# A transformer block on one Trainium2 core: gate 1 in four column groups per step, gate 2 summed by VectorE during the down projections

## The chip, the cores and the metric

The kernel runs on one core of one Trainium2 chip. The metric is the device time of one execution in microseconds (us); the kernel before took 1503.56 us, the median of three runs. The core has five instruction streams that matter here: PE (TensorE, the matrix engine; PEld is its weight load), DVE (VectorE), ACT (ScalarE), POOL (GpSimd) and SP, whose stream issues all the large loads from HBM.

## What is computed

One layer of a diffusion transformer on 256 latent tokens of width 2048, with 256 context tokens. A vector `c` gives six modulation vectors of 2048 each. The layer mixes the tokens by three branches (hyena, retention, S5), projects the result, adds it through gate `m_lat[2]`, and then does the same with a convolutional feed-forward network (FFN) through gate `m_lat[5]`:

```python
m_lat = jnp.split((jax.nn.silu(c) @ ada_w[i] + ada_b[i])[:, None, :], N_MOD, axis=-1)
a_lat = _modulate(h_lat, norm1_g[i], m_lat[0], m_lat[1]) @ w_in[i]
...
mix_l = jnp.concatenate([hyena_l, retention_l, s5_l], axis=-1) @ w_out[i]
h_lat = h_lat + m_lat[2] * mix_l
h_lat = h_lat + m_lat[5] * _conv_ffn(_modulate(h_lat, norm2_g[i], m_lat[3], m_lat[4]), ...)
return _rmsnorm(h_lat, norm_f)
```

`ada_w` has 2048 rows and 6 x 2048 columns. Of its six chunks of 2048 columns the first two are used for norm 1. The other four are what the change is about: `m_lat[2]` is chunk 0 of the kernel's `ada25` (gate 1), `m_lat[3]` and `m_lat[4]` are chunks 1 and 2 (shift and scale of norm 2), and `m_lat[5]` is chunk 3 (gate 2).

## The kernel before

Activations lie with features on the 128 partitions and the 256 tokens along the free dimension. All weights are float32 and come in blocks of 256 rows by 512 columns (512 KB). Each block is loaded by SP into a page of the ring `raw`, cast by ACT to its high part in a page of the ring `wh` (L454), and the remainder is taken by DVE into a page of `wl` (L456, called the split below). PE then makes three products per tile (L461, L462, L463: high by high, high by low, low by high), 24 matmuls of 256 columns per block in the usual case.

The order of work is this. Norm 1 and the S5 input come first, as the first two chunks of the modulation arrive (L373). Then follow keys and values with the S5 scan beside them, gate and queries, the three hyena projections with retention and the hyena transforms beside them, the output projection by `w_out`, and the FFN. The FFN has 11 units; `up(u)` takes 16 blocks of `w_up`, and `down(g)` takes the blocks of `w_down` for a group of two units (16 blocks, the last group 8). `down` runs over four column groups `cg` of 512 output features. The FFN runs in the order up 0, up 1, up 2, down 0, up 3, up 4, down 1 and so on, with down 5 last. After each column group of `down`, four DVE operations multiply the sums in PSUM by gate 2 and add them to the residual `hres` (L1419).

The four later chunks are made by the task `t_ada` (`ada25`), a generator that is advanced by a rate after every weight block: RK and RV (2 and 3 steps) during keys and values, RG and RH (0.8) during gate, queries and hyena, RW (0.75) during the output projection, RF (0.8) in `up`. A chunk is 32 loads of 512 KB (16 row tiles, two halves). It is made in one of two ways. `ada_matmul` (chunks 0 and 3) keeps `silu(c)` as the weights, 32 columns wide, and streams the chunk through PE in float32: four products per row tile, one for each 32-partition group of one PSUM bank (L412). Its task yields after each half, so that two products are emitted at a step. `ada_vector` (chunks 1 and 2, the list ADV) lets DVE scale and add the rows' tiles (L428, L430) and needs PE for four products at the end (L435). Both end in `ada_store`: an ACT copy (L363), four transposes on PE (L397) and a DVE addition (L400) into `ada_cols`. The loads go through the ring `ada`, which has two pages from the keys on (the first entry of RN); `raw`, `wh` and `wl` have three pages then, and four in the FFN.

The text order is not the executed order. A scheduler takes the emitted operations with their priorities, simulates the engines and lays down one instruction order per engine; on the chip every engine and SP run in that order. The splits of the weights have priority (PW).

Of the kernel before, what the change touches and what calls it, by code (L numbers as in the profile page):

```python
# [16 lines left out]
P = 128  # L17
# [39 lines left out]
def _lay(i):  # L57
    """The inputs as the kernel reads them: slices, transposes and constants of the shapes."""
# [84 lines left out]
    # constants of the shapes  # L143
# [24 lines left out]
RN=[2,3,3,3];SA=40000;SF=30000;R0=10;R1=1;R2=1;RS=4;RK=2;RV=3;RG=.8;RH=.8;RW=.75;RF=.8;RT=1.2;RR=3;RY=.75;PR=500;ADV=[1,2];ORD=[0,1,2,3];RP=1.5;RQ=20;KS=5;PW=800;AR=[6,8,8,8,7,5,5,5];ZE=[1,3];VE=[0,1,3];UE=[1,3]  # L168
class _Pages:
    """Tags of fixed sizes in the slot pool, taken and given back in the order of the program."""  # L170
# [12 lines left out]
class _Ring:  # L183
    """Tags taken in turn."""
# [9 lines left out]
class _Task:  # L194
    """Work that is emitted piece by piece between the blocks of the large products."""
# [23 lines left out]
def tile_dit(ctx: ExitStack, tc: tile.TileContext, I, out: bass.AP, dbg=None):  # L219
# [14 lines left out]
    @contextmanager  # L234
    def stream(name, start):
        """Instructions whose order of priority starts at -start and goes on from use to use."""
        n = counts.get(name, 0)
        with tc.high_priority(offset=tc.cur_priority + start - n):
            before = tc.cur_priority
            yield  # L240
            counts[name] = n + tc.cur_priority - before
# [4 lines left out]
    def resize(kind, n):  # L246
        """A ring of n pages of 4 KB."""
# [58 lines left out]
    def sum_squares(ps, sq, first, last):  # L306
        """Sums over the partitions and parts of sq [P, n, w], a token on each partition."""
# [6 lines left out]
    def inv_rms(ps, n, w):  # L314
        """1/sqrt(sum/n + eps) of w tokens' sums, on all partitions."""
# [76 lines left out]
    def ada_store(c, ps):  # L392
        """Four rows of 512 columns to their places."""
# [10 lines left out]
    def ada_matmul(c):  # L404
        """2048 of the modulation's columns for the latents, as products of TensorE."""
        ps = ada_bank()
        for kt in range(KT):
            raw = [load_a(I["ada25"][c, kt, half]) for half in range(2)]
            for half in (1, 0):
                for e in range(2):  # L410
                    q = 2 * half + e
                    T.matmul(ps[32 * q:32 * q + 32, :], cs[:, kt, :], raw[half][:, e, :],  # L412
                             start=(kt == 0), stop=(kt == KT - 1), skip_group_check=True)
                if (kt, half) != (KT - 1, 0):
                    yield
# [3 lines left out]
    def ada_vector(c):  # L419
        """The same, summed over the rows' tiles by VectorE and over partitions by TensorE."""  # L420
        ps = ada_bank()
        for half in range(2):
            tag = pages.take(4)
            acc = slot(tag, [P, 2, 512])
            for kt in range(KT):
# [5 lines left out]
                if kt < KT - 1:  # L431
                    yield
            for e in range(2):
# [4 lines left out]
            if half == 0:  # L438
                yield
# [3 lines left out]
    def ada25():  # L443
        """The other four chunks of the modulation (2048 columns each), for the latents."""
        for c in ORD:
            yield from (ada_vector if c in ADV else ada_matmul)(c)

# [11 lines left out]
    def prod(ps, a, b, first, last):  # L459
        """ps += a.T @ b with a = (high, low), b = (high, low)."""  # L460
# [12 lines left out]
    def feat_block(src, k0, at, mv, first, last):  # L473
        """256 rows of the weights into 512 features' sums: a bank's first start clears it for both."""
# [27 lines left out]
    def hyena_filters():  # L502
# [36 lines left out]
        for o in range(2):  # L539
            # even and odd parts of the filter's lags  # L540
# [833 lines left out]
    def with_ada():  # L1374
        t_ada.run(RF)
# [99 lines left out]
```

## Time and profile before

| | us |
|---|---|
| runs | 1507.85, 1503.56, 1503.34 |
| median of the runs | 1503.56 |
| profiled execution: its span | 1506.4 |
| PE busy | 1459.1 (97%) |
| DVE busy | 1040.6 (69%) |
| ACT busy | 658.0 (44%) |
| matmuls of L412 (chunks 0 and 3), busy | 62.7 |
| DVE sums of L430 (chunks 1 and 2), busy | 76.8 |

The profile gives the span of its execution and no time around it; that span is 2.8 us (0.2%) above the median of the runs. Busy time of an engine is the union of its instructions; a matmul's recorded duration overlaps that of the next one, so the pace of PE is read from starts, not from durations. A float32 product stands in the trace as two matmuls, and in the order of instructions as one row. The profile's chain is the sequence of work that ended last, followed back from the end.

### The profile page before, as it was taken

The numbers are of one execution on the slowest core, as the hardware profiler recorded it, in microseconds if no ns is written. First come the engines' busy times: TensorE is split into PE (matmuls) and PEld (weight loads), VectorE is DVE, ScalarE is ACT, GpSimd is POOL, SyncE is SP. The second block draws the span as 40 slices with busy tenths as digits, with TensorE's granted clock in tenths as the row PEclk, the third lists the DMA queues.
The fourth block names the chain that finished last, engine by engine and source line by source line (L and its number), as shares of the span: only waits on it lengthen the run. The fifth ranks groups of instructions, "written<-read, shape, count | busy, mean of one in ns | idle before, by whom it ended". The sixth has DMA issues, their size and how long they took to land.

```text
span 1506.4 us, 27320 instructions
## 1 busy us (share of the span) xinstructions
PE 1459.1 (97%) x11180; PEld 1314.7 (87%) x11180; DVE 1040.6 (69%) x1772; ACT 658.0 (44%) x974; POOL 10.9 (1%) x9
## 2 busy tenths in 40 slices
PE   6998999999999999999999999999999999999997
PEld 3566687678888987788899999999999999999997
DVE  6579519897869887653777665775667577657756
ACT  6337741213576433232554443443444344434434
POOL 0000000000000000000000000000000000000000
PEclk9999999999999999999999999999999999999998
DMA  9788635568877887677465666556665666656562
GB/s 352 260 313 291 229 101 197 183 194 278 281 252 253 299 303 261 219 226 251 145 182 183 185 182 184 185 177 192 183 183 182 182 183 183 185 183 184 178 189 90
DMA packets 89956, 318.58 MB, mean 211 GB/s; under 512 B 12039, under 2 KB 12584, under 8 KB 89384
## 3 DMA queue, kind: packets, MB, share of 16 engines
q1 hardware_dynamic: 89832, 316.85, 65.4%
q8 instruction: 87, 1.43, 0.4%
q14 instruction: 37, 0.30, 0.1%
HBM read 312.62 MB, written 4.19 MB: 210 GB/s over the span
## 4 chain that ended last, share of the span: by engine, by line
PE 83%; DVE 7%; DMA 5%; ACT 3%; issue 1%; SPq 0%; DVEq 0%; ACTq 0%
PE mm L461 24%; PE mm L462 23%; PE mm L463 23%; DMA s4k<-in_ada_dram 4%; PE ad L412 4%; DVE s4k L456 1%; DVE s4k L430 1%; PE sm L852 1%; PE ad L373 1%; PE sm L576 1%; PE mm L339 1%; PE sm L546 1%; DMA s4k<-in_x_t_dram 1%; PE sm L1158 0%; PE sm L1164 0%
## 5 line engine op out<-in xcount | busy, mean ns | idle before, releaser
L456 DVE TENSOR_TENSOR s4k<-s4k,s4k 128x1024 fp32r<-128x1024 f32 x376 | 459.6, 1223 | 324.1 <-ACT s4k L454 300.5
L454 ACT CAST s4k<-s4k 128x1024 fp32r<-128x1024 f32 x376 | 393.8, 1048 | 654.7 <-PE mm L462 483.3
L462 PE MATMUL mm<-s4k,s4k 128*128 128x256 f32 (+1 forms) x2144 | 629.0, 294 | 1.5 <-DVE s4k L775 1.2
L461 PE MATMUL mm<-s4k,s4k 128*128 128x256 f32 (+1 forms) x2144 | 626.9, 295 | 3.5 <-ACT s4k L454 3.1
L463 PE MATMUL mm<-s4k,s4k 128*128 128x256 f32 (+1 forms) x2144 | 624.7, 294 | 3.2 <-DVE s4k L456 3.2
L461 PEld LDWEIGHTS mm<-s4k,s4k 128*128 128x128 f32 x2144 | 411.9, 193 | 27.3 <-issue 12.9
L462 PEld LDWEIGHTS mm<-s4k,s4k 128*128 128x128 f32 x2144 | 414.3, 193 | 18.4 <-issue 8.2
L463 PEld LDWEIGHTS mm<-s4k,s4k 128*128 128x128 f32 x2144 | 412.1, 193 | 17.2 <-issue 6.9
L461 PE MATMUL mm<-s8k,s4k 128*128 128x256 f32 x960 | 272.7, 285 | 0.0
L462 PE MATMUL mm<-s8k,s4k 128*128 128x256 f32 x960 | 271.7, 284 | 0.0
L463 PE MATMUL mm<-s8k,s4k 128*128 128x256 f32 x960 | 271.1, 284 | 0.0
L461 PEld LDWEIGHTS mm<-s8k,s4k 128*128 128x128 f32 x960 | 183.9, 192 | 14.4 <-issue 12.6
L463 PEld LDWEIGHTS mm<-s8k,s4k 128*128 128x128 f32 x960 | 183.7, 192 | 4.3 <-issue 3.4
L462 PEld LDWEIGHTS mm<-s8k,s4k 128*128 128x128 f32 x960 | 184.3, 192 | 2.7 <-issue 2.5
L1396 DVE SCALAR_TENSOR_TENSOR t<-mm,s4k,t 128x189 f32<-128x189 f32 (+2 forms) x352 | 131.9, 424 | 7.9 <-ACT t L1388 6.3
L430 DVE SCALAR_TENSOR_TENSOR s4k<-s4k,cs,s4k 128x1024 f32<-128x1024 f32 x60 | 76.8, 1280 | 21.0 <-DMA s4k<-in_ada_dram 20.4
L412 PE MATMUL ad<-s4k,cs 128*32 128x512 f32 x256 | 62.7, 612 | 1.0 <-DMA s4k<-in_ada_dram 1.0
L1419 DVE SCALAR_TENSOR_TENSOR s4k<-mm,ada_cols,s4k 128x256 f32<-128x256 f32 x96 | 39.9, 477 | 4.7 <-PE mm L463 4.7
L373 PE MATMUL ad<-s4k,cs 128*32 128x256 f32 x512 | 35.6, 392 | 4.7 <-DMA s4k<-in_ada_dram 4.0
L1388 ACT ACTIVATE t<-mm,s4k 128x256 f32<-128x256 f32 x44 | 24.7, 562 | 14.6 <-PE mm L463 13.6
L466 ACT CAST s8k<-t 128x512 fp32r<-128x512 f32 x38 | 23.0, 616 | 18.2 <-DVE t L1403 9.3
L373 PEld LDWEIGHTS ad<-s4k,cs 128*32 128x32 f32 x512 | 13.8, 110 | 19.1 <-DMA s4k<-in_ada_dram 5.7
(281 smaller groups left out, 1023.5 us busy)
## 6 DMA issues: line engine op xcount, KB each, us to landing
s4k<-in_ada_dram SPq DMA_DIRECT2D x192, 512.0 KB, 4.9
s4k<-in_w_up_dram SPq DMA_DIRECT2D x176, 512.0 KB, 3.7
s4k<-in_w_down_dram SPq DMA_DIRECT2D x88, 512.0 KB, 3.7
s4k<-in_w_in_dram SPq DMA_DIRECT2D x80, 512.0 KB, 4.9
s4k<-in_w_out_dram SPq DMA_DIRECT2D x32, 512.0 KB, 4.6
s4k<-in_x_t_dram SPq DMA_DIRECT2D x8, 512.0 KB, 6.6
s4k<-in_ctx_t_dram SPq DMA_DIRECT2D x4, 512.0 KB, 10.2
hyk<-s8k SPq DMA_DIRECT2D x4, 512.0 KB, 4.0
```

What stands on the lines that cost most here:

```text
L373: T.matmul(ps[32 * q:32 * q + 32, :], cs[:, 2 * k2 + e, :], raw[:, e, 256 * part:256 * part + 256], start=(k2 == 0), stop=(k2 == 7), skip_ ...
L412: T.matmul(ps[32 * q:32 * q + 32, :], cs[:, kt, :], raw[half][:, e, :], start=(kt == 0), stop=(kt == KT - 1), skip_group_check=True)
L430: V.scalar_tensor_tensor(acc, raw, cs[:, kt, 0:1], acc, ALU.mult, ALU.add)
L454: S.copy(h, raw)
L456: V.tensor_tensor(lo, raw, h.bitcast(F32), ALU.subtract)
L461: T.matmul(ps, a[0], b[0], start=first, stop=False, skip_group_check=True)
L462: T.matmul(ps, a[0], b[1], start=False, stop=False, skip_group_check=True)
L463: T.matmul(ps, a[1], b[0], start=False, stop=last, skip_group_check=True)
L466: S.copy(h, src)
L1388: S.activation(acc[:, e, :], at(m), AF.Identity, bias=cw[:, 9, mt:mt + 1], scale=cw[:, 4, mt:mt + 1])
L1396: V.scalar_tensor_tensor(dst[:, r0:r1, c0:c1], src[:, r0 + dy:r1 + dy, c0 + dx:c1 + dx], cw[:, tap, mt:mt + 1], dst[:, r0:r1, c0:c1], ALU. ...
L1419: V.scalar_tensor_tensor(h_of(mt), at(m), ada_cols[:, 3, mt:mt + 1], h_of(mt), ALU.mult, ALU.add)
```

## The change

Four things are changed; comments and doc strings are dropped besides.

- Chunk 0 (`ada_matmul`) emits the four products of a row tile together, in the order of the column groups 0 to 3, and yields twice.
- Chunk 3 leaves `t_ada`, which makes chunks 0 to 2 alone and is finished ahead of the second norm. Chunk 3 is now a task of its own, `t_gate`, made by `ada_vector` on DVE, advanced by RD = 0.5 after each block of `down`. A one-element copy from `dsum` ties its sums to the first result of down 0. `ada_vector` yields twice more between its last sum and its products.
- The results of down 0 to down 4 are no longer gated one by one. Down 0's are copied by ACT into two buffers `dsum` of 8 KB per partition, those of down 1 to 4 are added to them by DVE, 512 columns at a time. Ahead of down 5 the sums are gated once, in 16 DVE operations; down 5 is gated as before.
- Retention emits the score products of both heads of a pair together, alternating between the two halves of the partitions, into two PSUM banks.

```diff
 def ada_matmul(c):
-            for half in (1, 0):
-                for e in range(2):
-                    q = 2 * half + e
-                    T.matmul(ps[32 * q:32 * q + 32, :], cs[:, kt, :], raw[half][:, e, :], ...)
-                if (kt, half) != (KT - 1, 0):
-                    yield
+            for q in range(4):
+                T.matmul(ps[32 * q:32 * q + 32, :], cs[:, kt, :], raw[q // 2][:, q % 2, :], ...)
+            if kt < KT - 1:
+                yield
+                yield
+        yield
...
-    def ada_vector(c):
+    def ada_vector(c, after=None):
...
+            if after is not None:
+                V.tensor_copy(acc[:, 0, 0:1], after)
...
+            yield
+            yield
...
-        for c in ORD:
+        for c in range(3):
...
+            pss = [sm_bank(), sm_bank()]
+            for s in range(2):
+                for e in range(2):
+                    ph = slice(64 * e, 64 * e + 64)
+                    T.matmul(pss[e][:, L * s:L * s + L], k_t[ph, pr, 128 * s:128 * s + 128], q_t[ph, pr, :], ...)
...
+    t_ada.finish()
     r = inv_rms(sums, D, L)
...
+    dsum = [slot(pages.take(8), [P, 8, L]) for _ in range(2)]
...
-    def with_ada():
-        t_ada.run(RF)
+    t_gate = _Task(ada_vector(3, dsum[0][:, 0, 0:1]))
+    def with_down(g, cg):
+        if (g, cg) != (0, 0):
+            t_gate.run(RD)
+    def gated(cg):
+        for mt in range(4 * cg, 4 * cg + 4):
+            V.scalar_tensor_tensor(h_of(mt), dsum[cg // 2][:, mt % 8, :], ada_cols[:, 3, mt:mt + 1], h_of(mt), ...)
...
-            bk, at = gemm_feat(I["w_down"], cg, mv, lambda: None, kcs)
+            bk, at = gemm_feat(I["w_down"], cg, mv, lambda: with_down(g, cg), kcs)
+            if finish is None:
+                for pr in range(2):
+                    k0 = 4 * (cg % 2) + 2 * pr
+                    acc = dsum[cg // 2][:, k0:k0 + 2, :].rearrange("p m n -> p (m n)")
+                    if g == 0:
+                        S.copy(acc, bk[pr])
+                    else:
+                        V.tensor_tensor(acc, acc, bk[pr], ALU.add)
+                continue
...
-            up(n, with_ada)
+            up(n, lambda: None)
         else:
+            if n == len(groups) - 1:
+                t_gate.finish()
+                for cg in range(4):
+                    gated(cg)
```

In the changed kernel the split is L459, the three products are L464 to L466, chunk 0's products L410, the DVE sums L433, the products behind them L440. Three places of the instruction orders follow, before and after; names before the arrow are written, those behind it read, and the numbers belong to buffers (`ad` is the PSUM bank of the modulation, `mm` that of a projection, `sm` that of a transform, `s4k` and `s8k` pages).

On PE, a row tile of chunk 0 during keys and values, before:

```order
L412 MATMUL ad_1937<-s4k_286_2330,cs 32x512 x2
L461 MATMUL mm_1814<-s4k_187_1415,s4k_288_2338 128x256
L462 MATMUL mm_1814<-s4k_188_1416,s4k_288_2338 128x256
L463 MATMUL mm_1814<-s4k_187_1415,s4k_289_2340 128x256
L461 MATMUL mm_1814<-s4k_187_1415,s4k_288_2338 128x256
L462 MATMUL mm_1814<-s4k_188_1416,s4k_288_2338 128x256
L463 MATMUL mm_1814<-s4k_187_1415,s4k_289_2340 128x256
L461 MATMUL mm_1815<-s4k_187_1415,s4k_288_2338 128x256
L412 MATMUL ad_1937<-s4k_285_2328,cs 32x512 x2
```

On PE, the same row tile in the changed kernel:

```order
L410 MATMUL ad_1937<-s4k_285_2328,cs 32x512 x2
L464 MATMUL mm_1814<-s4k_187_1415,s4k_288_2338 128x256
L465 MATMUL mm_1814<-s4k_188_1416,s4k_288_2338 128x256
L466 MATMUL mm_1814<-s4k_187_1415,s4k_289_2340 128x256
L464 MATMUL mm_1814<-s4k_187_1415,s4k_288_2338 128x256
L465 MATMUL mm_1814<-s4k_188_1416,s4k_288_2338 128x256
L466 MATMUL mm_1814<-s4k_187_1415,s4k_289_2340 128x256
L410 MATMUL ad_1937<-s4k_286_2330,cs 32x512 x2
```

The two halves of the tile have changed places, and there are six products of the projection between them instead of seven.

On PE, the end of the last hyena transform (`sm`) and the first block of `w_out` that reads its result (`s8k_719`), before:

```order
L461 MATMUL sm_5802<-s4k_714_5038,s8k_717_5043 128x256
L462 MATMUL sm_5802<-s4k_715_5039,s8k_717_5043 128x256
L463 MATMUL sm_5802<-s4k_714_5038,s8k_718_5044 128x256
L412 MATMUL ad_5435<-s4k_886_6325,cs 32x512 x2
L412 MATMUL ad_5435<-s4k_885_6323,cs 32x512 x2
L461 MATMUL mm_5767<-s8k_719_5045,s4k_877_6233 128x256
L461 MATMUL mm_5768<-s8k_719_5045,s4k_877_6233 128x256
```

On PE, the same place in the changed kernel (the result is `s8k_715` there):

```order
L464 MATMUL sm_5777<-s4k_710_5026,s8k_713_5031 128x256
L465 MATMUL sm_5777<-s4k_711_5027,s8k_713_5031 128x256
L466 MATMUL sm_5777<-s4k_710_5026,s8k_714_5032 128x256
L464 MATMUL mm_5742<-s8k_715_5033,s4k_860_6170 128x256
L464 MATMUL mm_5743<-s8k_715_5033,s4k_860_6170 128x256
```

Chunk 3's four products no longer stand between the transform and the projection.

On DVE, the end of the first column group of down 0, before:

```order
L456 TENSOR_TENSOR s4k_1184_8826<-s4k_1182_8822,s4k_1183_8824 128x1024
L1419 SCALAR_TENSOR_TENSOR s4k_817_5758<-mm_8634,ada_cols,s4k_817_5758 128x256 x2
L1419 SCALAR_TENSOR_TENSOR s4k_817_5758<-mm_8635,ada_cols,s4k_817_5758 128x256 x2
L456 TENSOR_TENSOR s4k_1187_8856<-s4k_1185_8852,s4k_1186_8854 128x1024
L456 TENSOR_TENSOR s4k_1192_8892<-s4k_1190_8888,s4k_1191_8890 128x1024
```

On DVE, the same place in the changed kernel (`s8k_959` is the first buffer `dsum`, `s4k_1150` the sum of chunk 3):

```order
L459 TENSOR_TENSOR s4k_1154_8695<-s4k_1152_8691,s4k_1153_8693 128x1024
L427 COPY s4k_1150_8686<-s8k_959_6903 128x1
L431 TENSOR_SCALAR s4k_1150_8686<-s4k_1151_8688,cs 128x1024
L459 TENSOR_TENSOR s4k_1157_8725<-s4k_1155_8721,s4k_1156_8723 128x1024
L433 SCALAR_TENSOR_TENSOR s4k_1150_8686<-s4k_1158_8751,cs,s4k_1150_8686 128x1024
L459 TENSOR_TENSOR s4k_1163_8762<-s4k_1161_8758,s4k_1162_8760 128x1024
L433 SCALAR_TENSOR_TENSOR s4k_1150_8686<-s4k_1167_8818,cs,s4k_1150_8686 128x1024
```

The gating is gone from here, and chunk 3's sums stand one by one between the splits.

## Rows read from the trace of the kernel before

**Rows 1.** The profile's chain that ended last, shares by line

```profile
PE mm L461 24%; PE mm L462 23%; PE mm L463 23%; DMA s4k<-in_ada_dram 4%; PE ad L412 4%; DVE s4k L456 1%; DVE s4k L430 1%; PE sm L852 1%; PE ad L373 1%; PE sm L576 1%; PE mm L339 1%; PE sm L546 1%; DMA s4k<-in_x_t_dram 1%; PE sm L1158 0%; PE sm L1164 0%
```

**Rows 2.** Busy time by stage: length; PE, PEld, DVE, ACT, POOL; clock, DMA share, GB/s

```profile
566.00:721.00 155.00, 154.63 (x1085) 124.26 (x1083) 87.19 (x123) 50.24 (x62) 0.00 (x0) 1.00 0.72 236
...
735.00:1480.00 745.00, 745.00 (x6211) 745.00 (x6209) 507.72 (x756) 325.31 (x362) 0.00 (x0) 1.00 0.60 181
```

**Rows 3.** The first of these stages, L412 alone: PE, PEld, clock, DMA

```profile
566.00:721.00 155.00, 30.52 (x116) 4.19 (x116) 1.00 0.72 236
```

**Rows 4.** Timeline of PE around one pair: start, us, engine, line, tile, form, count

```profile
627.43 0.28 PE L463 MATMUL mm<-s8k,s4k 128*128 128x256 f32 x1
627.63 1.05 PE L412 MATMUL ad<-s4k,cs 128*32 128x512 f32 x4
628.62 0.38 PE L461 MATMUL mm<-s8k,s4k 128*128 128x256 f32 x1
628.84 0.28 PE L462 MATMUL mm<-s8k,s4k 128*128 128x256 f32 x1
628.96 0.28 PE L463 MATMUL mm<-s8k,s4k 128*128 128x256 f32 x1
```

**Rows 5.** Timeline of PE: two pairs that stand together

```profile
576.20 1.07 PE L412 MATMUL ad<-s4k,cs 128*32 128x512 f32 x8
```

**Rows 6.** Timeline: last transform to first dependent block of the output projection

```profile
648.09 1.05 PE L412 MATMUL ad<-s4k,cs 128*32 128x512 f32 x4
...
648.27 0.62 ACT L466 CAST s8k<-t 128x512 fp32r<-128x512 f32 x1 [6.49 <-DVE t L1258]
...
650.49 0.75 PE L461 MATMUL mm<-s8k,s4k 128*128 128x256 f32 x4
```

**Rows 7.** Timeline of PE at the end of the output projection

```profile
722.58 1.05 PE L412 MATMUL ad<-s4k,cs 128*32 128x512 f32 x4 [0.42 <-DMA s4k<-in_ada_dram]
...
726.62 1.05 PE L412 MATMUL ad<-s4k,cs 128*32 128x512 f32 x4 [0.21 <-DMA s4k<-in_ada_dram]
727.60 1.10 PE L321 MATMUL sm<-ident,t 128*128 128x128 f32 x4
728.50 1.06 PE L397 MATMUL ad<-ident,s4k 128*128 128x128 f32 x4
```

**Rows 8.** Groups by line, 735 to 1480 us: busy, mean ns, idle before

```profile
L456 DVE TENSOR_TENSOR s4k<-s4k,s4k 128x1024 fp32r<-128x1024 f32 x258 | 316.0, 1225 | 226.8 <-ACT s4k L454 225.3
...
L1419 DVE SCALAR_TENSOR_TENSOR s4k<-mm,ada_cols,s4k 128x256 f32<-128x256 f32 x84 | 34.8, 477 | 0.0
...
L1403 DVE TENSOR_TENSOR t<-t,mm 128x512 f32<-128x512 f32 x22 | 14.9, 678 | 0.0
```

**Rows 9.** Groups by line, whole span: the sums of chunks 1 and 2

```profile
L430 DVE SCALAR_TENSOR_TENSOR s4k<-s4k,cs,s4k 128x1024 f32<-128x1024 f32 x60 | 76.8, 1280 | 21.0 <-DMA s4k<-in_ada_dram 20.4
```

**Rows 10.** Timeline of DVE: sums of chunk 2 among splits

```profile
511.92 1.28 DVE L430 SCALAR_TENSOR_TENSOR s4k<-s4k,cs,s4k 128x1024 f32<-128x1024 f32 x1
...
521.53 1.29 DVE L430 SCALAR_TENSOR_TENSOR s4k<-s4k,cs,s4k 128x1024 f32<-128x1024 f32 x1 [0.26 <-DMA s4k<-in_ada_dram]
...
529.17 1.28 DVE L430 SCALAR_TENSOR_TENSOR s4k<-s4k,cs,s4k 128x1024 f32<-128x1024 f32 x1 [0.61 <-DMA s4k<-in_ada_dram]
```

**Rows 11.** DMA issues, 480 to 566 us, then 735 to 1480: KB each, median us to landing

```profile
s4k<-in_ada_dram SPq DMA_DIRECT2D x22, 512.0 KB, 5.1
...
s4k<-in_w_down_dram SPq DMA_DIRECT2D x88, 512.0 KB, 3.7
```

**Rows 12.** Ten us with dense DMA, columns as in rows 2

```profile
560.00:570.00 10.00, 10.00 (x77) 8.87 (x76) 4.76 (x9) 5.24 (x8) 0.00 (x0) 1.00 0.99 355
```

**Rows 13.** Timeline: DVE between the last hyena transforms, and PE's use of it

```profile
624.53 0.69 DVE L1228 TENSOR_TENSOR t<-sm,s8k 128x512 f32<-128x512 f32 x1 [2.74 <-PE sm L463]
...
638.85 1.29 DVE L467 TENSOR_TENSOR s8k<-t,s8k 128x512 fp32r<-128x512 f32 x2
...
641.69 0.38 PE L461 MATMUL sm<-s4k,s8k 128*128 128x256 f32 x1
```

More of the change, by code (lines that the diff above doesn't have):

```diff
@@ L165, in _lay @@
     return o
-RN=[2,3,3,3];SA=40000;SF=30000;R0=10;R1=1;R2=1;RS=4;RK=2;RV=3;RG=.8;RH=.8;RW=.75;RF=.8;RT=1.2;RR=3;RY=.75;PR=500;ADV=[1,2];ORD=[0,1,2,3];RP=1.5;RQ=20;KS=5;PW=800;AR=[6,8,8,8,7,5,5,5];ZE=[1,3];VE=[0,1,3];UE=[1,3]
+RN=[2,3,3,3];SA=40000;SF=30000;R0=10;R1=1;R2=1;RS=4;RK=2;RV=3;RG=.8;RH=.8;RW=.75;RD=.5;RT=1.2;RR=3;RY=.75;PR=500;ADV=[1,2];RP=1.5;RQ=20;KS=5;PW=800;AR=[6,8,8,8,7,5,5,5];ZE=[1,3];VE=[0,1,3];UE=[1,3]
 class _Pages:
@@ L408, in ada_matmul @@
             raw = [load_a(I["ada25"][c, kt, half]) for half in range(2)]
-            for half in (1, 0):
-                for e in range(2):
-                    q = 2 * half + e
-                    T.matmul(ps[32 * q:32 * q + 32, :], cs[:, kt, :], raw[half][:, e, :],
-                             start=(kt == 0), stop=(kt == KT - 1), skip_group_check=True)
-                if (kt, half) != (KT - 1, 0):
-                    yield
+            for q in range(4):
+                T.matmul(ps[32 * q:32 * q + 32, :], cs[:, kt, :], raw[q // 2][:, q % 2, :],
+                         start=(kt == 0), stop=(kt == KT - 1), skip_group_check=True)
+            if kt < KT - 1:
+                yield
+                yield
+        yield
         ada_store(c, ps)
         yield
-    def ada_vector(c):
+    def ada_vector(c, after=None):
         ps = ada_bank()
@@ L437, in ada_vector @@
             pages.give(tag)
-            if half == 0:
-                yield
         ada_store(c, ps)
@@ L1152, in retention @@
             yb = sm_bank()
+            pss = [sm_bank(), sm_bank()]
+            for s in range(2):
+                for e in range(2):
+                    ph = slice(64 * e, 64 * e + 64)
+                    T.matmul(pss[e][:, L * s:L * s + L], k_t[ph, pr, 128 * s:128 * s + 128], q_t[ph, pr, :],
+                             start=True, stop=True)
             for e in range(2):
                 hd = 2 * pr + e
-                ph = slice(64 * e, 64 * e + 64)
-                ps = sm_bank()
-                for s in range(2):
-                    T.matmul(ps[:, L * s:L * s + L], k_t[ph, pr, 128 * s:128 * s + 128], q_t[ph, pr, :],
-                             start=True, stop=True)
+                ps = pss[e]
                 dm = dmat[:, hd, :]
@@ L1372, in hidden @@
         return hid[u]
-    def with_ada():
-        t_ada.run(RF)
+    t_gate = _Task(ada_vector(3, dsum[0][:, 0, 0:1]))
[4 more added lines that the diff above has]
+        for mt in range(4 * cg, 4 * cg + 4):
+            V.scalar_tensor_tensor(h_of(mt), dsum[cg // 2][:, mt % 8, :], ada_cols[:, 3, mt:mt + 1], h_of(mt),
+                                   ALU.mult, ALU.add)
     def up(u, between):
```

## The prediction

> **What bounds the kernel now.** I read the chain first. Seventy per cent of the span lies on the three products of the weight blocks, 4% on L412, the products of the modulation's chunks 0 and 3, and 1% each on the splits and on the DVE sums [rows 1]. So PE sets the end, and L412 is paid for there. Next come the stages. While chunk 3 is made (566 to 721 us: the end of hyena and the output projection) PE is busy 154.6 of 155 us and DVE 87.2; in the FFN PE is busy all of 745 us and DVE 507.7 [rows 2]. There 6211 matmuls in 745 us give a pace of 0.12 us, and 24 of them a block in 2.88 us. Third, what L412 costs in its place. Around one pair PE's starts run 627.43, 627.63, 628.62, 628.84, 628.96 [rows 4]; the products around the pair would start 0.12 apart, so that 628.84 would be 627.67 without it. **One run of L412 costs 1.17 us.** Two pairs that stand together are recorded with 1.07 us, where one pair has 1.05 [rows 4, 5]: four column groups cost what two cost. What counts is how many separate runs stand in PE's order.
>
> **Chunk 3 leaves PE.** In 566 to 721 us there are 116 matmuls of L412, busy 30.5 us [rows 3]; at 1.05 us a run that is 29 runs. At 1.17 us each they take 33.9 us of a PE that hardly waits there. Not all of it comes back. At 648.09 two runs stand between the last transform and the first product that reads its result at 650.49, but that result's high part was only cast from 648.27 to 648.89 [rows 6]. Without them PE would start at about 649.0 and would then wait a little for the low part: some 1.3 of these 2.4 us remain as waiting. That leaves 32.6 us. The last runs lie at the end of the output projection, where PE has little else to do; only the one at 726.62 stands in the way, of the broadcast at 727.60, which could have started 0.6 us earlier [rows 7]. Together: **-33.2 us**.
>
> **Chunk 0 with four column groups.** Emitted together they could be 16 runs instead of many. In the order before I count 26 runs of L412 for chunk 0, in the changed order 27 of L410: the two halves of a tile arrive by separate loads, and the scheduler again puts projection products between them, as the first place of the order shows. PE gets them in that order. One run more is **+1.2 us**.
>
> Here a rule speaks for more. The Trainium skill, "TensorE: Matmul & The Clock Gate", section "Part 3: Packing small matmuls", says that matmuls on different column groups run at once, so that a pack takes little longer than one of them. The trace agrees, 1.07 against 1.05 us. Read alone it would promise 16 runs for 26 or 27, 12 to 13 us; the order withholds that, so it is a rival below and no term of the sum.
>
> **Chunk 3 on VectorE, in the FFN.** PE gets two runs of two products each (L440, 512 columns as L412: 2.3 us by rows 4) and four transposes, which the order has moved from the end of the output projection into down 4. They are recorded with 1.06 us [rows 7], part of it overlap; I take 0.7. **+3.0 us** of PE.
>
> DVE gets 32 sums of 1.28 us [rows 9], 41 us at most. It loses the gating of down 0 to 4, 80 operations of 477 ns (38 us), and gets 32 additions of 512 columns from PSUM (678 ns, as L1403, 21.7 us) and 16 late gatings (at most 477 ns, 7.6 us) [rows 8]. Net some 32 us on top of 507.7 in 745: 72% instead of 68%. The eight copies of down 0 go to ACT, busy 325 of 745 [rows 2]. As a total this is no bound. As order it may be one: the sums don't spread as RD says, but stand in two stretches of 16, each one by one between splits (the third place of the order), 17 splits in the first and 16 in the second.
>
> What hides them is the lead of the weights. The FFN has four pages of high and low parts, so the cast of a block starts when PE has finished the block four before it, three blocks (8.64 us) ahead of its use; cast and split take 2.3 us, which leaves **6.3 us of slack**. Against it stands the ring of two pages for the chunk. A load can start only when the sum two before has ended, and needs 5.1 us to land [rows 11] (3.7 in the FFN's lighter traffic), so two sums take at least 6.4 us, 3.2 each. In chunk 2 five intervals take 17.25 us, 3.45 each, with waits for the load, and the longest two 7.64 (521.53 to 529.17), 3.82 each [rows 10]. DVE works in order, so a late load holds up the splits behind it. A stretch is then 15 intervals: 48 us at 3.2, 51.8 at 3.45, 57.3 at 3.82, where PE uses 17 splits in 49.0 us and 16 in 46.1. The first stretch starts some 4 us late, because the one-element copy waits for ACT's copy behind the first column group with a split queued behind it; the second some 2 us, behind the additions. Lateness beyond 6.3 us stops PE: nothing at 3.2; 51.8 - 49.0 + 4 - 6.3 = 0.5 and 51.8 - 46.1 + 2 - 6.3 = 1.4 at 3.45; 6.0 and 6.9 at 3.82. I take 3.45, as it is the mean of the row with sums and splits mixed: **+2 us**, bounds 0 and 13. The rate of the loads itself is no tighter: a weight block and a chunk's tile are 1.05 MB, 2.95 us at 355 GB/s [rows 12].
>
> **The late gating** needs chunk 3's transposes, which stand in PE's order 91 products (10.9 us) ahead of the first use of the next split queued behind the gating on DVE. Ahead of that split DVE has ten gatings and two additions, 6.1 us, and the split is 1.2: hidden, with 3 us left. If that cover fails, at most the 6.1 us show. The end of the kernel is unchanged.
>
> **Retention.** Its products stand in 14 runs instead of 12. A run's two edges cost about 0.1 us each beyond the usual 0.12 [rows 4], 0.4 us in all; four of 32 score products can now overlap, which may save about as much. I take 0, bounds -1.5 and +1.5.
>
> **The sum.** -33.2 + 1.2 + 3.0 + 2 = **-27.0 us**. On the profiled span, 1506.4, that gives 1479.4; that span is 2.8 us above the median of the runs, so the forecast is 1503.6 - 27.0 = **1476.6 us**.
>
> **The rivals.**
> - *The transforms become the bound.* Between 624.53 and 640.14 DVE makes the spectrum's products, and PE takes the result at 641.69 [rows 13]; three runs of L412 (3.5 us) filled that time, five (5.9 us) the same place of the first transform. Without them PE could wait there up to 2 and 4 us. Against it: the scheduler has put 16 more products of the projection between transform and inverse, 1.9 us, and weights are ready. Price 6: 1483.
> - *The ring of two pages paces the FFN*, at 3.82 us a sum: 13 instead of 2 us, 1488. For it speaks that the FFN asks for one tile per 2.88 us, more than chunk 2 ever got over five sums; against it that landing times are short again as soon as the stretch lags.
> - *Gate 1 does pack*, 16 runs: 11 x 1.17 = 12.9 us less, 1463.7. It needs PE to bring the halves together against its order; rows 4 and the other runs with single products between them show nothing of that.
> - *Slower.* The same ring at 4.6 us a sum: 69 - 49.0 + 4 - 6.3 = 17.7 and 69 - 46.1 + 2 - 6.3 = 18.6, together 36.3 against the 29.0 that all else brings: 1511. From about 4.2 us a sum the whole gain is gone; the slowest two in rows 10 had 3.82.
> - *Nothing changes*: the ring at 4.1 to 4.4 us a sum.
>
> **How the numbers follow.** Chances: the forecast with its bounds (1470 to 1483) 0.60, the transforms 0.12, the ring 0.17, packing 0.04, slower 0.04, nothing 0.03. About 0.3%, 4.5 us, is what a measurement of this kernel can tell from no change. Faster by more than that is 0.60 + 0.12 + 0.17 + 0.04 = 0.93, the same 0.03, slower 0.04. The range goes from 1465 (bounds of retention, the transition and the ring at their best, 1468, and part of packing) to 1491 (the ring case and some waiting at the transforms).
>
> **What would show it.** In the profile after: L410 with 128 matmuls in 27 or so runs of 1.05 us; no such product between 570 and 725 us, and the FFN starting some 32 us earlier; in the FFN PE busy all the time, or with waits for L459 late in two stretches of about 50 us, at down 0 and down 2; sums of L433 3.2 to 3.5 us apart, each with a short wait for its load; additions of about 0.68 us. The prediction is wrong if chunk 0's runs are far from 27, if the stage without chunk 3 doesn't shrink by about 32 us, or if the FFN grows by more than 10.

## The result, and the profile after

| | before | changed |
|---|---|---|
| median of the runs, us | 1504.85 | 1480.81 |
| profiled execution: its span, us | 1506.4 | 1484.0 |
| ratio of the times, 95% interval | | 0.9833 (0.9809 to 0.9858) |

The changed kernel is 25 us faster (21 to 29); forecast were 27.0, and 1476.6 us in a range of 1465 to 1491. Measured again beside the experiments it gave 1479.39 us and a ratio of 0.9835 (0.9810 to 0.9861). The total is right. Of its terms some are, and the others were off by amounts that cancel.

First the chain of the changed kernel, shares of the span by line, against [rows 1]:

```profile
PE mm L464 24%; PE mm L465 24%; PE mm L466 24%; DMA s4k<-in_ada_dram 6%; PE ad L410 2%; PE ad L373 2%; DVE s4k L433 1%; PE sm L579 1%; DVE s4k L459 1%; PE sm L855 1%; PE mm L339 1%; PE sm L311 1%; PE sm L549 1%; ACT s4k L457 1%; DMA s4k<-in_x_t_dram 1%
```

PE still sets the end; the modulation's products have gone from 4% to 2%, which is chunk 0 alone.

Second, chunk 0's products on PE in the changed kernel (start, us, line, form, count), against [rows 4, 5]:

```profile
223.25 1.07 PE L410 MATMUL ad<-s4k,cs 128*32 128x512 f32 x8
...
230.96 1.05 PE L410 MATMUL ad<-s4k,cs 128*32 128x512 f32 x4
...
232.85 1.05 PE L410 MATMUL ad<-s4k,cs 128*32 128x512 f32 x4
```

There are 27 such groups. Most halves of a row tile still stand apart, as the order said.

Third, the FFN. Here is the stage by windows, columns as in [rows 2], then the costliest new groups on DVE in it, as in [rows 8]:

```profile
735.00:1460.00 725.00, 725.00 (x6033) 723.06 (x6033) 521.24 (x729) 317.04 (x353) 0.00 (x0) 1.00 0.64 203
```

```profile
L433 DVE SCALAR_TENSOR_TENSOR s4k<-s4k,cs,s4k 128x1024 f32<-128x1024 f32 x30 | 38.5, 1282 | 17.8 <-DMA s4k<-in_ada_dram 17.7
L1439 DVE TENSOR_TENSOR s8k<-s8k,mm 128x512 f32<-128x512 f32 x32 | 21.8, 685 | 0.4
...
L1389 DVE SCALAR_TENSOR_TENSOR s4k<-s8k,ada_cols,s4k 128x256 f32<-128x256 f32 x16 | 6.8, 478 | 0.0
```

PE is busy for all of the 725 us, though DVE waits 17.7 us for chunk 3's loads. Durations are the forecast's: 1.28, 0.69 and 0.48 us. The timeline of DVE shows the two stretches of sums (first and last of each, and the sum with the longest wait):

```profile
857.86 0.75 DVE L431 TENSOR_SCALAR s4k<-s4k,cs 128x1024 f32<-128x1024 f32 x1
...
905.95 1.28 DVE L433 SCALAR_TENSOR_TENSOR s4k<-s4k,cs,s4k 128x1024 f32<-128x1024 f32 x1
...
1135.03 0.75 DVE L431 TENSOR_SCALAR s4k<-s4k,cs 128x1024 f32<-128x1024 f32 x1
...
1171.37 1.28 DVE L433 SCALAR_TENSOR_TENSOR s4k<-s4k,cs,s4k 128x1024 f32<-128x1024 f32 x1 [3.37 <-DMA s4k<-in_ada_dram]
...
1185.40 1.28 DVE L433 SCALAR_TENSOR_TENSOR s4k<-s4k,cs,s4k 128x1024 f32<-128x1024 f32 x1
```

Fifteen intervals take 48.1 and 50.4 us, 3.2 and 3.4 us a sum, and even a wait of 3.37 us ahead of one sum doesn't reach PE.

### Where the time went

The two traces can't be laid side by side by time, because PE's order has changed. So I compare them **at equal work**: in each trace I add up the columns of the matmuls that both kernels have, in the order of their starts, without the products of chunks 0 to 3 (L410 or L412, L435 or L440, and the transposes L397), and read off when the same sum is reached. The difference is how far PE is behind (+) or ahead (-) of the kernel before. The stages of the table are those of the kernel before: 200 to 340 us holds most of chunk 0, 340 to 560 the gate, the queries and most of hyena, 560 to 740 the end of hyena, the output projection and norm 2, then the FFN. Each cell is the change within the stage, in us.

| kernel | ratio | 0-200 | 200-340 | 340-560 | 560-740 | 740-end |
|---|---|---|---|---|---|---|
| forecast for the change | 0.982 | 0 | +1.2 | 0 | -33.2 | +5.0 |
| changed, first profile | 0.9833 | 0.0 | +0.8 | +6.7 | -32.0 | +2.8 |
| e1 changed, again | 0.9835 | -7.0 | +1.0 | +5.8 | -31.8 | +2.8 |
| e2 without the retention edit | 0.9873 | -6.5 | +1.0 | +3.1 | -24.1 | +2.8 |
| e3 without the gate 1 edit | 0.9836 | -1.1 | +0.1 | +6.4 | -33.5 | +2.8 |
| e4 chunk 0 by one load a tile | 0.9855 | -6.4 | -9.4 | +15.4 | -28.8 | +2.8 |
| e5 gate 2 part alone | 0.9879 | +0.9 | -0.4 | +3.2 | -24.1 | +2.5 |
| e6 before, without chunk 3 | 0.9854 | +1.7 | -0.9 | +1.4 | -25.1 | -0.1 |
| e7 old steps of chunks 1, 2 | 0.9840 | -1.6 | +0.8 | +3.7 | -30.6 | +2.8 |
| e8 chunk 0 by four pages | 0.9866 | +1.4 | -2.8 | +11.8 | -32.4 | +2.8 |
| e9 e4 with hyena's rate 1 | 0.9817 | -7.0 | -9.4 | +11.9 | -30.9 | +2.9 |
| e10 changed, hyena's rate 1 | 0.9845 | -1.3 | +0.8 | +6.6 | -27.7 | +2.6 |
| e11 retention edit alone | 1.0001 | -4.5 | -0.5 | +3.2 | -2.4 | +0.1 |
| e12 e4 with slower steps | 0.9840 | -5.2 | -9.2 | +12.1 | -25.9 | +2.9 |

The first stage differs by up to 9 us from one execution to the next, also where no edit reaches it (e11 edits only what comes after 340 us). From 200 us on equal orders agree within 1 us or so (the first profile, e1, e3 and e10 between 340 and 560 us, e2 and e5 in both stages from there to 740). The ratios rest on many runs, the cells on one execution each.

### The profile page after: what moved, and what is told of

Its sections match the earlier page's. It is cut to its first block, busy times and chain, and to the rows that moved or that the text cites. A ratio compares the mean times of both kernels' runs of the same rounds, so it can differ in the third digit from the quotient of the medians.

```text
span 1484.0 us, 27112 instructions
## 1 busy us (share of the span) xinstructions
PE 1429.8 (96%) x11060; PEld 1314.1 (89%) x11060; DVE 1070.7 (72%) x1774; ACT 664.5 (45%) x984; POOL 10.9 (1%) x9
## 4 chain that ended last, share of the span: by engine, by line
PE 82%; DMA 7%; DVE 5%; ACT 3%; issue 2%; SPq 0%; DVEq 0%; ACTq 0%
PE mm L464 24%; PE mm L465 24%; PE mm L466 24%; DMA s4k<-in_ada_dram 6%; PE ad L410 2%; PE ad L373 2%; DVE s4k L433 1%; PE sm L579 1%; DVE s4k L459 1%; PE sm L855 1%; PE mm L339 1%; PE sm L311 1%; PE sm L549 1%; ACT s4k L457 1%; DMA s4k<-in_x_t_dram 1%
## 5 line engine op out<-in xcount | busy, mean ns | idle before, releaser
L459 DVE TENSOR_TENSOR s4k<-s4k,s4k 128x1024 fp32r<-128x1024 f32 x376 | 459.0, 1222 | 252.8 <-ACT s4k L457 247.9
L464 PE MATMUL mm<-s4k,s4k 128*128 128x256 f32 (+1 forms) x2144 | 627.3, 295 | 4.8 <-ACT s4k L457 3.5
L466 PE MATMUL mm<-s4k,s4k 128*128 128x256 f32 (+1 forms) x2144 | 626.1, 294 | 4.9 <-DVE s4k L459 4.9
L464 PEld LDWEIGHTS mm<-s4k,s4k 128*128 128x128 f32 x2144 | 412.2, 193 | 28.9 <-issue 14.8
L466 PEld LDWEIGHTS mm<-s4k,s4k 128*128 128x128 f32 x2144 | 412.9, 193 | 19.9 <-DVE s4k L459 7.4
L464 PE MATMUL mm<-s8k,s4k 128*128 128x256 f32 x960 | 271.0, 283 | 0.8 <-ACT s8k L469 0.8
L466 PE MATMUL mm<-s8k,s4k 128*128 128x256 f32 x960 | 269.9, 283 | 0.0
L464 PEld LDWEIGHTS mm<-s8k,s4k 128*128 128x128 f32 x960 | 183.9, 192 | 3.6 <-issue 2.5
L466 PEld LDWEIGHTS mm<-s8k,s4k 128*128 128x128 f32 x960 | 183.5, 192 | 0.1
L433 DVE SCALAR_TENSOR_TENSOR s4k<-s4k,cs,s4k 128x1024 f32<-128x1024 f32 x90 | 115.4, 1282 | 49.2 <-DMA s4k<-in_ada_dram 48.8
L1403 ACT ACTIVATE t<-mm,s4k 128x256 f32<-128x256 f32 x44 | 24.7, 562 | 14.6 <-PE mm L466 13.6
L410 PE MATMUL ad<-s4k,cs 128*32 128x512 f32 x128 | 28.9, 604 | 1.0 <-DMA s4k<-in_ada_dram 0.5
L470 DVE TENSOR_TENSOR s8k<-t,s8k 128x512 fp32r<-128x512 f32 x38 | 25.8, 686 | 1.0
```

Of the source, the lines that this page charges most:

```text
L410: T.matmul(ps[32 * q:32 * q + 32, :], cs[:, kt, :], raw[q // 2][:, q % 2, :], start=(kt == 0), stop=(kt == KT - 1), skip_group_check=True)
L433: V.scalar_tensor_tensor(acc, raw, cs[:, kt, 0:1], acc, ALU.mult, ALU.add)
L459: V.tensor_tensor(lo, raw, h.bitcast(F32), ALU.subtract)
L464: T.matmul(ps, a[0], b[0], start=first, stop=False, skip_group_check=True)
L466: T.matmul(ps, a[1], b[0], start=False, stop=last, skip_group_check=True)
L470: V.tensor_tensor(lo, src, h.bitcast(F32), ALU.subtract)
```

## The experiments

### e1 and e2: the changed kernel again, and without the retention edit

No edit in e1. In e2:

```diff
-            pss = [sm_bank(), sm_bank()]
-            for s in range(2):
-                for e in range(2):
-                    ...
-                    T.matmul(pss[e][:, L * s:L * s + L], k_t[ph, pr, ...], q_t[ph, pr, :], ...)
...
-                ps = pss[e]
+                ps = sm_bank()
+                for s in range(2):
+                    T.matmul(ps[:, L * s:L * s + L], k_t[ph, pr, ...], q_t[ph, pr, :], ...)
```

> The changed kernel once more, unaltered, beside the kernel before. In the first profile PE was behind the kernel before by 7 us of equal work at 560 us, of which the sum had only 1.2 (chunk 0's 27th run); the rest stood as waits of some 3 us and as stretches with a granted clock of 0.74 to 0.92 around 360, 395, 440 and 455 us. If that loss belongs to the change, it stands here again: behind by 6 to 8 us at 560 us, ratio 0.984 to 0.986 (22 to 24 us faster). If it was that one execution, PE is behind by 1 to 3 us there, and the ratio is 0.980 to 0.983 (26 to 30 us).

> The changed kernel with retention's score products as they were before (one head after the other, one bank each). My theory, retention worth nothing: within 1.5 us of the changed kernel, and PE's lag at 560 us is the same. Rival, the extra lag between 340 and 560 us comes from the score products that now take two banks at once: 4 to 6 us faster than the changed kernel, with the lag at 560 us gone.

e1 gave 0.9835, between the two ranges that I had set: the loss between 340 and 560 us is the change's own (+5.8 after +6.7), and the lead that hid it comes from the first 200 us. e2 gave 1485.88 us, 0.9873 (0.9850 to 0.9895), where I expected either nothing or a gain: **undoing the retention edit cost 6.5 us** between the medians. (0.0038 of the ratio is 5.7 us, and the cells from 200 us on differ by 5 us, so 5 to 6.5.) It does take away 3 us of the loss between 340 and 560, as the rival had it, but gives back 8 us behind. What PE waited for in e2 between 565 and 640 us (us in total, times, longest):

```profile
PE sm L464 <- ACT s8k L469: 3.5, 2, 1.9
PE sm L466 <- DVE s8k L470: 0.8, 1, 0.8
PE mm L464 <- ACT s8k L469: 0.8, 1, 0.8
```

The changed kernel has only the last of these there. They belong to the last hyena transform, here on PE's timeline in e2:

```profile
619.88 0.39 PE L466 MATMUL sm<-s4k,s4k 128*128 128x512 f32 x1
...
622.92 0.39 PE L464 MATMUL sm<-s4k,s8k 128*128 128x256 f32 x1 [1.58 <-ACT s8k L469]
...
624.47 0.50 PE L466 MATMUL sm<-s4k,s8k 128*128 128x256 f32 x2 [0.82 <-DVE s8k L470]
626.92 0.54 PE L464 MATMUL sm<-s4k,s8k 128*128 128x256 f32 x1 [1.95 <-ACT s8k L469]
627.26 0.42 PE L465 MATMUL sm<-s4k,s8k 128*128 128x256 f32 x1
627.47 0.42 PE L464 MATMUL sm<-s4k,s8k 128*128 128x256 f32 x1
...
634.51 0.74 PE L464 MATMUL mm<-s8k,s4k 128*128 128x256 f32 x4 [0.79 <-ACT s8k L469]
```

From 622.92 on these are the 48 products of the inverse transform (other orders part them into 10 and 38). In e2 they stand in one run, and PE waits three times in it: for a high part, for a low part, and at 626.92 for the next high part. In the changed kernel the same stretch, from the last forward product at 619.82 to the projection at 636.46, holds 81 products of the output projection (e2: 9), and PE waits for nothing in it but the last 0.79 us.

### e5, e6, e11: the parts alone

e5 is the kernel before with the gate 2 part alone, e11 with the retention edit alone; e6 leaves chunk 3 out of the kernel before:

```diff
-ORD=[0,1,2,3]
+ORD=[0,1,2]
...
-                V.scalar_tensor_tensor(h_of(mt), at(m), ada_cols[:, 3, mt:mt + 1], h_of(mt), ALU.mult, ALU.add)
+                V.scalar_tensor_tensor(h_of(mt), at(m), ada_cols[:, 0, mt:mt + 1], h_of(mt), ALU.mult, ALU.add)
```

> The kernel before with the gate 2 part alone (chunk 3 on VectorE in the FFN, down sums gated once); chunk 0 and retention as before. Theory, gate 1 is worth nothing and the retention edit helps only through the order: in this order, as in the one without the retention edit, the last hyena transform's 10 and 38 products stand in one run of 48 with no projection product between, and PE waits some 5 us there. So 18 to 21 us faster than the kernel before, ratio 0.986 to 0.988. Rival, the parts add up by their own costs (retention's products themselves slower one head at a time): the same total, but the waits at the last transform stay below 1 us and the 5 us are found between 480 and 565 us.

> The kernel before with chunk 3 of the modulation left out (its 32 loads and 64 products; the FFN's result is gated by chunk 0's row instead). It gives the price that chunk 3 had on TensorE. My sum: 33.2 us less, 1472 us, with the FFN's length unchanged. Rival, the transforms become the bound without those products as cover: its order has the last transform's products in one run of 48, so PE waits 4 to 6 us there, and 27 to 29 us are left, 1476 to 1478 us.

> The kernel before with the retention edit alone. Undoing that edit cost the changed kernel 6 us, without a change in chunk 0 or 3. Theory, the edit itself is worth nothing and what it moved was the place of the last transform's products: here both orders keep other products at that place (26 and 38 products stand alone), chunk 3's among them, so the same as before within 2 us, with PE some 3 us later around 560 us and that back by 660. Rival, the edit saves products or waits of its own: 4 to 6 us faster than before.

e5: 1487.22 us, 0.9879 (0.9855 to 0.9903), as the theory had it; the 4.3 us of waits at the last transform are there. e11: 1507.05 us, 1.0001 (0.9982 to 1.0019): the edit by itself is worth nothing. It loses 3.2 us before 560 us and gets 2.4 back behind.

e6: 1484.41 us, 0.9854 (0.9836 to 0.9872). **Without chunk 3 the kernel before is only 22 us faster (19 to 25), not 33.** Even the rival (27 to 29) was too high. PE's waits from 565 to 730 us tell why, first in the kernel before, then in e6:

```profile
PE ad L412 <- DMA s4k<-in_ada_dram: 1.0, 3, 0.4
PE mm L461 <- ACT s4k L1355: 0.3, 1, 0.3
```

```profile
PE sm L461 <- ACT s8k L466: 3.1, 1, 3.1
PE sm L311 <- DVE s4k L1321: 2.2, 1, 2.2
PE mm L461 <- ACT s4k L1355: 1.1, 1, 1.1
PE mm L461 <- ACT s8k L466: 0.8, 1, 0.8
PE sm L461 <- DVE t L1229: 0.6, 1, 0.6
PE sm L321 <- DVE t L318: 0.6, 1, 0.6
PE mm L462 <- DVE s4k L1356: 0.2, 1, 0.2
```

With chunk 3 PE waited 1.3 us in this stretch; without it 8.6. Its products had filled the time in which ACT and DVE finish the transforms (L466, L1229) and norm 2 (L1321, L1355, L318). These waits are 7.3 us; missing are 8 by the table (-25.1 for the stage) and 11 by the runs. Part of the rest is the granted clock. In this stage it fell to 0.50 once in the kernel before, at norm 2, and twice in e6, behind the transform's waits and at norm 2 (columns as in [rows 2]; first the kernel before, then e6):

```profile
727.80:734.60 6.80, 6.22 (x27) 5.52 (x27) 5.85 (x16) 4.03 (x9) 0.00 (x0) 0.50 0.01 4
```

```profile
630.20:637.00 6.80, 6.14 (x28) 6.14 (x29) 1.85 (x3) 1.21 (x2) 0.00 (x0) 0.50 0.20 75
701.90:712.10 10.20, 8.23 (x36) 7.56 (x36) 6.85 (x18) 4.04 (x10) 0.00 (x0) 0.50 0.17 52
```

PE is busy for 8 us more at this clock, at which products of 256 columns start 0.21 us apart instead of 0.12. By my estimate from these figures that is some 3.5 us.

Where nothing is awaited the price per run holds: in the output projection from 660 to 720 us the gain is 12.8 us in every kernel without chunk 3 but e12, and 11 runs at 1.17 us are 12.9.

### e9 and e10: one rate, two orders

Both have the modulation's steps in hyena at rate 1 instead of 0.8 (`RH`), e9 on top of e4, e10 on the changed kernel.

> The kernel with chunk 0's tiles in one load, and the modulation's steps during hyena at rate 1 instead of 0.8 (RH). That leaves the order up to hyena alone, and at the last transform it puts 8 projection products between its 10 and its 38 products, which stood in one run of 48. Theory, the run of 48 costs 4 to 5 us of waiting: 4 to 5 us faster than that kernel (1483.1), about 1478.5, with the 2.9 us wait at the last transform gone. Rival, the run of 48 is only where a wait shows that any order has: the same time, with the wait at another place between 565 and 640 us.

> The changed kernel with the same rate 1 instead of 0.8. Here it does the opposite to the order: the 8 projection products ahead of the last transform's 38 go away and 46 stand in one run. Theory: 4 to 5 us slower than the changed kernel (1479.4), some 1484, with a wait of some 3 us for ScalarE's high part there. Rival: the same time within 1.5 us.

e9: 1477.32 us against e4's 1483.10, and e4's wait of 2.9 us at this place is gone (0.2 left). In e4 it was:

```profile
PE sm L468 <- ACT s8k L473: 2.9, 1, 2.9
```

e10: 1484.25 us against the changed kernel's 1479.39, with waits of 1.5 and 0.9 us at the last transform:

```profile
PE sm L464 <- ACT s8k L469: 1.5, 1, 1.5
PE sm L466 <- DVE s8k L470: 0.9, 1, 0.9
PE mm L464 <- ACT s8k L469: 0.8, 1, 0.8
```

By the medians the same edit gains 5.8 us where it separates the run and loses 4.9 where it joins it; by the table's cells from 200 us on it is 5.5 and 4.3. The ratios are less sure: 0.9855 to 0.9817 is 5.7 us, but 0.9835 to 0.9845 is only 1.5, and the intervals of either pair overlap, so the times alone don't exclude e10's rival. With the waits that go and come at this place, the place of those products is a cause, not only where a wait happens to be seen, and the retention edit's 5 to 6.5 us are of this kind: no work was saved, the scheduler laid down another order. One reservation: of e9's gain over e4 only 2.1 us lie between 560 and 740 us. Another 3.5 us lie between 340 and 560, most of them in hyena, where the rate moves chunk 2's steps too; so this pair isn't the last transform alone.

### e3, e4, e8, e12: chunk 0

e3 emits chunk 0 as before. e4 loads a whole row tile (1 MB) at once into a free page of 8 KB, e8 keeps the loads and gives the ring four pages for chunk 0, e12 is e4 with the rates 0.5 and 0.6 instead of 0.8 (`RG`, `RH`). e4:

```diff
+        tag8 = pages.take(8)
         for kt in range(KT):
-            raw = [load_a(I["ada25"][c, kt, half]) for half in range(2)]
+            big = slot(tag8, [P, 2, 2, 512])
+            dma(big, I["ada25"][c, kt].rearrange("h p e n -> p h e n"))
+            raw = [big[:, half] for half in range(2)]
```

> The changed kernel with chunk 0 emitted as before, two products at a step. Its order has 26 runs of them instead of 27. My theory, a run costs 1.17 us whatever it holds: 1.2 us faster than the changed kernel, so the same within 1.5. Rival, the emission in fours brings the halves together on the chip after all: 3 us or more slower than the changed kernel.

> The changed kernel with each row tile of chunk 0 fetched by one load of 1 MB into a free page of 8 KB, so that its four products are ready at once: the order has 16 runs of four instead of 27. Theory, a run of four column groups costs what a run of two does: 11 x 1.17 = 12.9 us faster than the changed kernel, a run recorded with 1.05 to 1.1 us. Rival 1, four different column groups take twice as long as two: runs of 2 us and no gain. Rival 2, the one page is late: the load of a tile starts only when the tile before is used, and PE waits for it by a few us per tile, which eats the gain or more (0 to 30 us slower).

> The changed kernel with four pages instead of two in the modulation's ring while chunk 0 is made. Its order has 16 runs of chunk 0, some of two or three row tiles, together some 21 times four column groups instead of 27 runs. Theory: PE is 6 x 1.17 = 7 us ahead at 340 us; between there and 565 us the S5 chain on VectorE and ScalarE takes most of it back, as it did with the single load (where PE waited 4.9 and 2.9 us for ScalarE's copies of S5): 0 to 4 us faster than the changed kernel. Rival, the single load lost its gain only by the run of 48 at the last transform: then this kernel, with 11 products between, keeps it, 5 to 8 us faster.

> Chunk 0's tiles in one load, and the modulation's steps slower: rate 0.5 during gate and queries (RG, was 0.8) and 0.6 during hyena (RH). Chunk 2's sums on VectorE are spread from 440 to 580 us to some 440 to 650 us, where VectorE has room since chunk 3 is gone; the last transform's products stand apart, as with rate 1. It tests what takes back the single load's 11 us between 340 and 565 us. If VectorE's load by chunk 2's sums does: PE's loss of equal work between 420 and 565 us, 6 to 7 us with rate 1, falls to 2 to 4 us, and the time is 2 to 5 us under that kernel's 1477.3. If it is the S5 chain and chunk 1 (both untouched): no change beyond 2 us.

e3: 1480.34 us, 0.9836, the same as the changed kernel. The gate 1 edit does nothing; its one run more shows as +0.8 and +1.0 us against +0.1.

e4 has 16 runs of four column groups. Two of them on PE:

```profile
255.36 1.07 PE L413 MATMUL ad<-s8k,cs 128*32 128x512 f32 x8
...
265.20 1.07 PE L413 MATMUL ad<-s8k,cs 128*32 128x512 f32 x8
```

Four groups in 1.07 us: that part of the theory holds, and PE is 9.4 us further ahead at 340 us than at 200. Yet the kernel takes 1483.10 us, 0.9855 (0.9832 to 0.9879), no better than the changed one. The costliest waits of PE in e4 between 180 and 565 us:

```profile
PE sm L980 <- ACT s8k L935: 4.9, 5, 2.8
PE ad L413 <- DMA s8k<-in_ada_dram: 4.1, 3, 2.6
PE sm L1008 <- ACT s8k L993: 2.9, 1, 2.9
```

The single page costs 4.1 us (rival 2, in small). The rest of the gain is given back between 340 and 560 us, +15.4 against +6, where PE now waits 7.8 us for ACT's copies of the S5 chain (the waits of the list other than the loads; 2.5 us in the changed kernel), and then at the joined last transform. With that transform repaired (e9) this is the fastest kernel tried, 1477.32 us and 0.9817 (0.9788 to 0.9845); its interval overlaps that of the changed kernel. e8: 1486.73 us, 0.9866, the worst of the four: PE waited 4.0 us for the chunk's loads in the keys and values, gained 2.8 us there instead of 7, and lost 11.8 behind. My expectation for e8 failed with its rival.

e12 asked whether DVE's sums of chunk 2 take the gain back. Its rates moved only the second half of them, from 514 to 571 us in e9 to 536 to 597; the first half stands at 454 to 513 us (450 to 511 in e9). The half that moved doesn't take the gain back: +12.1 us between 340 and 560 us, as in e9, and 8 to 9 of them are lost before 480 us in both. Moved later, these sums stand ahead of DVE's part of the transforms instead, and PE waits there, between 565 and 640 us:

```profile
PE mm L468 <- DVE s4k L1295: 4.0, 1, 4.0
PE sm L468 <- DVE t L1238: 3.2, 1, 3.2
```

1483.80 us, 0.9840 (0.9822 to 0.9859), so neither of the times that I had expected. What takes back some 10 us of a faster chunk 0 is therefore not the later half of chunk 2. The S5 waits point to the S5 chain, but no run isolates it from chunk 1's sums, which fall into the same time, and it stays open.

### e7: the later steps of chunks 1 and 2

```diff
-            yield
-            yield
+            if after is not None:
+                yield
+                yield
...
+            if half == 0 and after is None:
+                yield
```

> The changed kernel with the steps of chunks 1 and 2 as they were (one step after the products of the first half, not two ahead of each half's products); chunk 3 keeps the new steps. It tests why PE loses 6 us of equal work between 340 and 565 us. If the later steps of chunks 1 and 2 do it: 3 to 6 us faster than the changed kernel, and that lag gone. If not: the same within 2 us. Its order keeps 11 projection products ahead of the last transform's 38, so no wait is due there.

1482.85 us, 0.9840 (0.9817 to 0.9863): not faster. The loss between 340 and 560 us falls from 6 to 3.7 us, but the next stage gains less, with one wait of 3.8 us for DVE's hyena convolution (L1294) that the changed kernel hasn't got. The steps are a part of the loss, and worth nothing.

## Why the prediction was right, and where its steps were not

**The price of a run** (1.17 us, whatever its number of column groups) was right: 12.8 us for 11 runs in the output projection, 1.07 us for four groups in e4, 2.8 us for the FFN's two runs and the transposes. The Trainium skill, "TensorE: Matmul & The Clock Gate", section "Part 3: Packing small matmuls", says as much of column groups, and e4's runs agree.

**Chunk 3 leaves PE, -33.2 us: too large.** The step that failed is "At 1.17 us each they take 33.9 us of a PE that hardly waits there". That PE didn't wait there was because the runs filled its waits; taken away, 8.6 us of waits stand in 565 to 730 us instead of 1.3 (e6), the clock falls for longer, and chunk 3's whole price was 22 us (19 to 25). I had left 1.3 us for it at the last transition and put the rest into the first rival, the transforms, at 6 us and 12%. That rival came true wherever the order joins the last transform (e2, e5, e6, e4, e10); the changed kernel escaped it, as the order that I had read ("16 more products of the projection between transform and inverse") said. Norm 2 I missed in every version:

```profile
696.79 1.39 PE L311 MATMUL sm<-ones,s4k 128*128 128x2 f32 x8 [2.17 <-DVE s4k L1326]
...
702.22 1.22 PE L321 MATMUL sm<-ident,t 128*128 128x128 f32 x4 [0.63 <-DVE t L318]
...
704.55 0.79 PE L464 MATMUL mm<-s4k,s4k 128*128 128x256 f32 x2 [1.11 <-ACT s4k L1361]
```

In the changed kernel's timeline these are waits of 3.9 us where [rows 7] had 0.6. The broadcast starts at 702.22 instead of 727.60, 25.4 us earlier and not 32. The clock makes norm 2 dearer still. From 690.0 to 697.3 us, with the first of these waits, PE is busy for 5.13 of 7.3 us; then the clock is granted at 0.50 for 13.7 us, against 6.8 us in the kernel before:

```profile
690.00:697.30 7.30, 5.13 (x44) 4.92 (x42) 7.28 (x13) 3.68 (x6) 0.00 (x0) 1.00 0.53 190
697.30:711.00 13.70, 11.72 (x52) 11.05 (x53) 8.27 (x22) 5.49 (x13) 0.00 (x0) 0.50 0.15 41
```

PE is busy 5.5 us more at this clock than before (11.72 against 6.22), which by the starts 0.21 and 0.12 us apart is some 2.4 us, an estimate. The sum had neither term.

**Retention, 0 with bounds of 1.5: right alone (e11), wrong in its place.** With the gate 2 part the edit is worth 5 to 6.5 us, because it moves the order of hyena. My sum took an order for the change as a whole, but priced the parts as if each kept its own.

**Between 340 and 560 us the sum had nothing, and PE loses 6 us.** About 3 of it belong to the retention edit (6.4 on average in the four profiles that have it with the new steps, 3.1 in e2 and e5, which don't have it) and some 2 to 3 to the later steps of chunks 1 and 2 (e7). The rest is no more than e6 shows with an order that is unchanged up to hyena (+1.4). Part of it is waiting and part is the clock: from 340 to 480 us the kernel before has a granted clock of 0.98, the changed one 0.95, which is 0.50 for 6.8 and for 13.7 us. These are the two stretches in the kernel before, then in the changed one:

```profile
340.00:480.00 140.00, 128.98 (x935) 120.75 (x934) 110.91 (x166) 83.63 (x146) 7.19 (x4) 0.98 0.80 267
480.00:565.00 85.00, 85.00 (x620) 77.60 (x619) 71.89 (x85) 31.18 (x39) 0.00 (x0) 1.00 0.88 295
```

```profile
340.00:480.00 140.00, 129.83 (x926) 121.70 (x925) 106.86 (x159) 85.02 (x147) 7.18 (x4) 0.95 0.77 259
480.00:565.00 85.00, 81.11 (x587) 74.38 (x586) 73.64 (x92) 30.91 (x40) 0.00 (x0) 1.00 0.82 280
```

**Gate 1, +1.2: right** (+0.8 and +1.0), and so was the reason, the order's 27 runs.

**The FFN: +3.0 of products was right (2.8), +2 of stalls was not (0).** I took 3.45 us a sum; it was 3.2 and 3.4, inside the bounds, and below what the lead of the weights covers. That decides against the rivals in which the ring paces the FFN.

So the forecast was near because misses cancelled, which is luck. By the runs of the parts, a term too large by 11 us stood against an order worth 6.5 us that I had priced at nothing, and 2.2 us too much in the FFN: -27.0 + 11 - 6.5 - 2.2 = -24.7, against 25 measured. Each of these differences is uncertain by some 3 us, so that they meet to 0.3 us says nothing. By the changed kernel's own stages it reads otherwise: 560 to 740 us shrank by 32, near the 33.2 that I had forecast. That its order fills the transforms with products of the projection, and regains there some of what it lost ahead of 560 us (as e11's -2.4 after +3.2), fits this, but no run prices it in this order. In this reading the misses are 6.2 us between 340 and 560, 1.3 in that stage, 0.3 less for gate 1 and 2.2 less in the FFN (means of the changed kernel's two profiles): -27.0 + 6.2 + 1.3 - 0.3 - 2.2 = -22.0 from 200 us on. None of the signs of a wrong prediction that I had named showed: there are 27 runs, that stage shrank by 32, the FFN grew by 2.8. Of what I had expected to see, only the FFN's start missed, 25 us earlier and not 32. As a reading of the kernel, the FFN, gate 1 and the output projection were understood; hyena and norm 2 were not.

## What to carry to other kernels

Work on the bounding engine that also fills its waits is worth less than its duration: before pricing its removal, list for each place what the engine would have waited for without it. In a kernel whose order a scheduler lays down, an edit can gain or lose several microseconds with no work of its own, so read the order at the places where the bounding engine depends on a chain through other engines, and try the edit with a neighbouring rate before crediting it. When orders differ, compare two traces at equal work, not at equal time.

## What the runs showed of the hardware

Three short waits in a row cost more than their sum. In e2, at the last transform, two windows of the profile show this (length, PE and PEld busy, ..., granted clock, DMA share, GB/s):

```profile
620.00:627.00 7.00, 2.65 (x18) 2.00 (x16) 6.92 (x12) 2.94 (x5) 0.00 (x0) 1.00 0.75 241
627.00:630.40 3.40, 3.40 (x16) 3.40 (x17) 1.20 (x2) 0.47 (x1) 0.00 (x0) 0.50 0.04 10
```

PE was busy 2.65 of 7 us, no single wait longer than 1.95 us, and the clock was then granted at 0.50, which is 1.2 GHz, for 3.4 us in which PE was busy throughout: products start 0.21 us apart (627.26, 627.47) instead of 0.12. By the rows (16 products, 0.09 us more each) that adds some 1.4 us to the 4.3 of waiting. The clock is at 0.50 for 3.4 us at the joined transform in e4 (from 627.2 us), e5 (632.7) and e10 (631.9) too; in the changed kernel, which doesn't wait there, the clock is 1.00 from 451.6 to 697.3 us.
